# Causal mask of attention scores added in VectorE's pass for the maximum, in one core's hybrid decoder layer

## The chip, the cores and the metric

The kernel runs on one core of one Trainium2 chip, as a single program. The metric is device time in microseconds (us), the median of several runs; lower is better. A core has five engines that run at the same time and hand work to one another through semaphores: TensorE (PE in the profile, with its weight loads as PEld), VectorE (DVE), ScalarE (ACT), GpSimd (POOL) and SyncE (SP, which here only issues transfers). TensorE writes its products into PSUM, a small memory of eight banks; the other working memory is SBUF.

## What is computed

One decoder layer for a sequence of 1024 tokens of width 1024, in fp32. After a norm, one projection feeds two groups of heads side by side. Group B (gated DeltaNet, four heads) is a chunked scan along the sequence and is not touched here. Group A is differential attention: four heads, each with two softmax maps over the same causal past, and the second map subtracted with a learned weight. Both outputs go through one output projection, are added to the input, and an MLP with squared ReLU follows. The attention, cut to what matters:

```python
s = jnp.einsum('bqhcd,bkhcd->bhcqk', qb, k, preferred_element_type=jnp.float32) * scale
causal = (start + jnp.arange(Q_BLOCK))[:, None] >= k_pos[None, :]
s = jnp.where(causal, s, jnp.finfo(jnp.float32).min)
p = jax.nn.softmax(s, axis=-1)
a = p[:, :, 0] - lam * p[:, :, 1]
return jnp.einsum('bhqk,bkhe->bqhe', a.astype(v.dtype), v)
```

q and k are RMS-normed over the 64 entries of each of their parts beforehand; each head's output is RMS-normed after.

## The kernel before

The work runs in stages: the projections of the DeltaNet group with its preparation (to about 250 us), then a long stretch in which several strands are interleaved (about 250 to 625 us), then the MLP (to the end). Products in fp32 are made of three products of rounded parts (`wH`/`hH` the high part, `wL`/`hL` the rest).

The interleaved stretch is where the change lies. Its strands are generators: `scan` and `scan_out` (DeltaNet), `da_units` (projections of q, k and v of the attention, 48 units of 24 matmuls into `ps_qk`, L1063 to L1065), `da_turns` (transposes of q and k, `ps_qkt`, L1024), `scores` (the softmax maps), `values` (transposes of the maps, L1230 into `ps_at`, and their product with v, L1242 into `ps_o`), `mix_loads` and `mixed` (transposes of the mixed rows, L298), and `outproj` (L1332 to L1334). A planner, the class `Interleave`, decides at build time which strand issues next. It keeps a clock of its own for TensorE (`flow.pe`) and estimated queues of VectorE, ScalarE and GpSimd (`flow.chain` with `vec`, `act`, `powr`), and it holds a PSUM bank until the chain that reads it should be done (`flow.hold`). A strand whose bank or operand isn't due yet steps back, and another goes. TensorE's instructions then stand in exactly that order. The orders of the other engines and of the transfers are made by the framework's scheduler around it. A few transfers are tied behind another instruction by hand (`tc.issue_after`).

One unit of `scores` is one head and one block of 128 queries (`tb`), 32 units in all; it has two maps. A map has n = 128 (tb + 1) keys, from 128 to 1024, in one or two pieces of up to 512 columns, each piece in a PSUM bank of the tile `ps_sc`. There are two such tiles (`qsc`, and `rsc` once the scan is over). For each piece two matmuls run (L1189 with `qa`, L1190 with `qb`), and in the last piece a third, L1192: identity times a triangle `caus` of 0 and -1e30, both bf16, which adds the causal mask to the last 128 columns. VectorE then reduces the map to the negated maximum `mx` (L1194). ScalarE takes the exponential out of PSUM into the SBUF tile `pexp`, with `mx` as bias and the row sum as a second output (L1198). After both maps VectorE combines them (L1205 to L1208), and the unit goes on the list `ready`; a new unit starts while at most two are on it (`AHEAD = 2`).

Two places put squares aside. In `da_units`, ScalarE squares the 256 columns of a unit of q or k into an SBUF tile `qsq` (L1081) and copies the unit to `qn` (L1082); VectorE sums the squares (L1084). The bank is booked as free after the copy. In `values`, ScalarE copies the product out (L1251), squares the copy into an SBUF tile `osq2` with the sum as second output (L1252), and the bank is booked as free after the copy. GpSimd raises the sums to the power -1/2 (L291) and issues the stores of the first two heads' outputs (`mixa_d`, L1258), from a tile `om` with two buffers.

Of the kernel before, what the change touches and what calls it, by code (L numbers as in the profile page):

```python
# [9 lines left out]
F32 = mybir.dt.float32  # L10
F32R = mybir.dt.float32r
BF16 = mybir.dt.bfloat16
AF = mybir.ActivationFunctionType
ALU = mybir.AluOpType
AX = mybir.AxisListType
# [3 lines left out]
P = 128  # L19
# [88 lines left out]
def act(n, accum=False):  # L108
    return "S", 55.0 + 0.83 * n + (93.0 if accum else 0.0)


def vec(n, extra=0.0):
    return "V", 68.0 + 1.045 * n + extra


def powr(n):
    return "G", 180.0 + 285.0 * n
# [3 lines left out]
def tile_hymba_layer(  # L121
# [7 lines left out]
    V, S, G, T = nc.vector, nc.scalar, nc.gpsimd, nc.tensor  # L129
# [349 lines left out]
    with tc.manual_schedule(engines={T.engine, V.engine, S.engine, G.engine}):  # L479
# [49 lines left out]
        for tb in range(3, NT):  # L529
            for u in range(2):  # L530
                nxt, at = spread_at.get((tb, u), (None, 0))
                z[tb, u] = z_mm(tb, u, *pools[tb], nxt, at)
                if nxt is not None:
# [4 lines left out]
                    if nxt in (4, 5):  # L538
                        b = {4: 5, 5: 7}[nxt]
                        z_root(b)  # L540
                        z_diag(b)
                    last = next(parts)
# [16 lines left out]
    identb = const.tile([P, P], BF16, name="identb")  # L559
# [3 lines left out]
    caus = const.tile([P, P], BF16, name="caus")  # L563
# [8 lines left out]
    ps = ph.tile([P, 512], F32, tag="ph", name="ps_pv")  # L572
# [40 lines left out]
    u, au, e, w1, lw, d1, z1 = (n32(n) for n in ("gu", "gau", "gte", "gw1", "glw", "gd1", "gz1"))  # L613
# [21 lines left out]
    ps = ph.tile([P, 512], F32, tag="ph", name="ps_g")  # L635
# [21 lines left out]
    def ta(name, bufs, dt=F32):  # L657
        return sa.tile([P, 512], dt, tag=name, name=name, bufs=bufs)
# [100 lines left out]
    for h, hf, y, th in skew(dn_proj(1)):  # L759
# [3 lines left out]
        ps = transposed(k2)  # L763
# [65 lines left out]
    for h, hf, q2 in skew(dn_proj(0)):  # L829
# [3 lines left out]
        ps = transposed(q2)  # L833
        psm = gram(k2, q2)
        sq = ta("kn", 2)
# [15 lines left out]
    for h, hf, v2 in skew(dn_proj(2)):  # L851
        ps = transposed(v2)
# [20 lines left out]
    ap = dctx.enter_context(tc.tile_pool(name="ap", bufs=1, **right))  # L873
    sdctx = ExitStack()
    sd = sdctx.enter_context(tc.tile_pool(name="sd", bufs=1, **right))
# [2 lines left out]
    qsc = scctx.enter_context(tc.tile_pool(name="qsc", bufs=1, space=PSUM, **right))  # L878

    flow = Interleave()  # L880

    def bank_tile(pool, res, name):
        return pool.tile([P, 512], F32, tag=f"{res[0]}{res[1]}", name=name)
# [153 lines left out]
    def da_units():  # L1037
        todo = [(g, kind) for g in range(2) for kind in (1, 0, 2)]

        w = load_unit(w_units[2 * todo[0][1] + todo[0][0]]), unit_time()  # L1040
        for g, kind in todo[1:]:
            quarters.plan(w_units[2 * kind + g])
        for k0 in (4, 0):
            for n in range(2):
                quarters.plan(w_halves[n], k0, 4)
        quarters.load()
        quarters.load()
        freed = [0.0, 0.0]
        n = 0
        for i, (g, kind) in enumerate(todo):  # L1050
            (wh, wl), wt = w
            for j in range(NT):
                tb = NT - 1 - j if i == len(todo) - 1 else j
                if j == 0:
                    if i + 1 < len(todo):
                        w = quarters.unit(256, KB)
                    else:
                        pre.append(quarters.unit(512, 4))
                sl = slice(tb * P, (tb + 1) * P)
                yield max(freed[n % 2], wt[0] if j == 0 else 0.0), None  # L1060
                ps = pj.tile([P, 512], F32, tag="pj", name="ps_qk")
                for k in range(KB):
                    T.matmul(ps[:, :256], hH[:, k, sl], wh[:, k, :], start=(k == 0), stop=False)  # L1063
                    T.matmul(ps[:, :256], hH[:, k, sl], wl[:, k, :], start=False, stop=False)  # L1064
                    T.matmul(ps[:, :256], hL[:, k, sl], wh[:, k, :], start=False, stop=(k == KB - 1))  # L1065
                    if k % 2 == 1:
                        flow.pe(6 * TR)
                        if k < KB - 1:
                            yield wt[k // 2 + 1], None
                while len(late) > 2:  # L1070
                    yield flow.now + 50, None
                qn = sd.tile([P, 256], F32, tag="qn", name="qn", bufs=4)
                if kind == 2:
                    newest["ACT"] = S.copy(qn, ps[:, :256])
                    st = nc.gpsimd.dma_start(v_d[g, tb], qn.rearrange("p (h e) -> p h e", h=2))
                    if g == 1:
                        prefetch_x()
                    freed[n % 2] = flow.chain(act(256))
                else:
                    sq = sd.tile([P, 256], F32, tag="qsq", name="qsq", bufs=1)  # L1080
                    S.activation(sq, ps[:, :256], AF.Square)  # L1081
                    newest["ACT"] = S.copy(qn, ps[:, :256])  # L1082
                    sn = sd.tile([P, 4], F32, tag="sn", name="sn", bufs=2)
                    V.tensor_reduce(sn, sq.rearrange("p (a d) -> p a d", d=DQK), axis=AX.X, op=ALU.add)  # L1084
                    rn = sd.tile([P, 4], F32, tag="rn", name="rn", bufs=2)
                    rstd(rn, sn, 1.0 / DQK, EPS, sd, "rnt", 4)
                    qv = qn.rearrange("p (a d) -> p a d", d=DQK)
                    V.tensor_tensor(qv, qv, rn.unsqueeze(2).broadcast_to([P, 4, DQK]), ALU.mult)
                    t = flow.chain(act(256))
                    freed[n % 2] = flow.chain(act(256), start=t - flow.HOP)  # L1090
                    t = flow.chain(vec(256), vec(4), powr(4), vec(256), start=t - flow.HOP)
                    late.append((g, kind, tb, qn, t))
                quarters.block()
                if i == len(todo) - 1:
                    over.add(tb)
                n += 1
                state["units"] = n
            if kind == 2:
                while state["turned"] < 2 * NT * (g + 1):
                    yield flow.now + 50, None  # L1100
                state["da"] = g + 1
                state["da_t"] = flow.now + 3000
        sdctx.close()
        pctx.close()
        state["proj"] = True
# [30 lines left out]
    def scores():  # L1136
# [6 lines left out]
        for u, (h, tb) in enumerate(order):  # L1143
# [8 lines left out]
            if h == 2 and h not in heads:  # L1152
                while state["turned"] < 3 * NT:
                    yield flow.now + 300, None
                ks = load_head(2, ap), load_head(3, pools["a2"])
# [15 lines left out]
            qa, qb = q  # L1171
            n = (tb + 1) * P
            npc = 1 if n <= 512 else 2
            pl = n // npc
            pe, ssum = [], ap.tile([P, 2], F32, tag="ssum", name="ssum", bufs=4)
            mx = ap.tile([P, 2], F32, tag="mx", name="mx", bufs=4)
            for m in range(2):
                nsc += 1
                if state["scan"] and nsc % 2:
                    name, sc = "rsc", pools["rsc"]  # L1180
                else:
                    name, sc = "qsc", qsc
                yield 0, name
                sc = sc.tile([P, 1024], F32, tag="sc", name="ps_sc")
                for pc in range(npc):
                    o = sc[:, 512 * pc:512 * pc + pl]
                    ks = KS[m][:, pc * pl:(pc + 1) * pl]
                    last = pc == npc - 1
                    T.matmul(o, qa[:, m, :], ks, start=True, stop=False)  # L1189
                    T.matmul(o, qb[:, m, :], ks, start=False, stop=not last)  # L1190
                    if last:
                        T.matmul(sc[:, 512 * pc + pl - P:512 * pc + pl], identb, caus, start=False, stop=True)  # L1192
                scv = sc.rearrange("p (a b) -> p a b", b=512)[:, :npc, :pl]
                V.tensor_reduce(mx[:, m:m + 1], scv, axis=AX.XY, op=ALU.max, negate=True)  # L1194
                npe += 1
                ep = pools["be"] if state["scan"] and npe % 3 == 0 else ae
                e = ep.tile([P, SEQ], F32, tag="pexp", name="pexp")
                S.activation(e[:, :n].rearrange("p (a b) -> p a b", a=npc), scv, AF.Exp, bias=mx[:, m:m + 1],  # L1198
                             accum_out=ssum[:, m:m + 1])
                flow.pe(2 * max(n / 2.4, 110.0) + 55)  # L1200
                t = flow.chain(vec(n), act(n, True))
                flow.hold(name, t)
                pe.append(e)
            ri = ap.tile([P, 2], F32, tag="ri", name="ri", bufs=4)
            V.reciprocal(ri, ssum)  # L1205
# [3 lines left out]
            t = flow.chain(vec(10), vec(1, 60), vec(n, 100), start=t - flow.HOP)  # L1209
# [4 lines left out]
    def values():  # L1214
        for _ in order:
# [9 lines left out]
            for g in range(0, tb + 1, 4):  # L1225
# [11 lines left out]
                t = flow.chain(act(ng * P))  # L1237
                flow.hold(r, t)
            r = yield from flow.bank("px", at=t)
            po = bank_tile(px, r, "ps_o")  # L1240
            for j in range(tb + 1):
                T.matmul(po[:, :P], ats[j // 4][:, (j % 4) * P:(j % 4 + 1) * P], vt[:, j, :],  # L1242
                         start=(j == 0), stop=(j == tb))
            if h < 2:
                om = ap.tile([P, P], F32, tag="om", name="om", bufs=2)
            else:

                om = rows_of[tb][:, h * P:(h + 1) * P]
            sq = ap.tile([P, P], F32, tag="osq2", name="osq2", bufs=1)
            so = ap.tile([P, 1], F32, tag="so2", name="so2", bufs=2)  # L1250
            S.copy(om, po[:, :P])  # L1251
            S.activation(sq, om, AF.Square, scale=ri[:, 0:1], accum_out=so)  # L1252
# [7 lines left out]
            t = flow.chain(act(P))  # L1260
            flow.hold(r, t)
            t = flow.chain(act(P, True), vec(1), powr(1), vec(1), vec(P, 60), start=t)
# [568 lines left out]
    last = u_raw(4)  # L1831
# [78 lines left out]
```

## Time and profile before

| | |
|---|---|
| Median of 3 runs | 1241.6 us (1239.6 to 1242.4) |
| Profiled execution: span from first to last instruction | 1237.3 us (no time of its own is given beside it) |
| TensorE busy | 1222.9 us, 99% |
| TensorE weight loads busy | 1053.6 us, 85% |
| VectorE busy | 824.9 us, 67% |
| ScalarE busy | 618.7 us, 50% |
| GpSimd busy | 154.6 us, 12% |
| The reduction L1194, 64 times | 47.4 us, 752 ns each |
| The exponential L1198, 64 times | 47.5 us, 743 ns each |

In the profile's rows, "L1194" is a line of the kernel, an arrow points from what is read to what is written, "x64" is a count. Rows of groups give busy time, mean duration in ns, and the idle time of the engine just before, with the instruction that ended it. Rows of the timeline give start and duration in us. Rows of waits give total, count and longest. Matmul rows overlap, as matmuls are pipelined: what one costs is seen from start to start. The granted clock of TensorE is 1.000 throughout.

### The profile page before, as it was taken

What the parts mean: (1) busy time and instruction counts of PE and PEld (TensorE: products, weight loads), DVE (VectorE), ACT (ScalarE), POOL (GpSimd) and SP (SyncE); (2) the same over time, 40 slices, a digit from 0 to 9 for tenths busy, and PEclk for the clock granted to TensorE, in tenths of its full rate; (3) what the DMA queues carried; (4) which work ended last, traced back from release to release, by engine and by line L of the source; (5) the groups of instructions that cost most, each with busy time, mean ns of one, the idle gap of its engine ahead of it and who ended that gap; (6) DMA issues with size and microseconds to landing.
All of it is one profiled execution on the core that took longest, in us unless ns stands there. A gap on an engine that the chain in (4) does not pass through costs nothing.

```text
span 1237.3 us, 18898 instructions
## 1 busy us (share of the span) xinstructions
PE 1222.9 (99%) x6887; PEld 1053.6 (85%) x6887; DVE 824.9 (67%) x1458; ACT 618.7 (50%) x1249; POOL 154.6 (12%) x215
## 2 busy tenths in 40 slices
PE   9999999999999999999999999999999999999998
PEld 8978888899998998888888888888888888888886
DVE  6868796566647656777689555566569755777543
ACT  6587554244445555566667444544564333333330
POOL 2411110034335421111200000000000000000000
PEclk9999999999999999999999999999999999999999
DMA  9344653179648755223346534444469655432301
GB/s 350 104 112 119 167 158 108 56 238 270 212 141 256 219 163 151 82 72 115 125 147 223 189 122 157 180 156 153 167 234 376 237 179 186 166 102 102 137 34 68
DMA packets 143301, 202.12 MB, mean 163 GB/s; under 512 B 20920, under 2 KB 98280, under 8 KB 143208
## 3 DMA queue, kind: packets, MB, share of 16 engines
q1 hardware_dynamic: 138584, 187.28, 46.6%
q0 software_dynamic: 4480, 13.64, 2.9%
q8 instruction: 54, 0.88, 0.3%
q14 instruction: 39, 0.32, 0.1%
q10 hardware_dynamic: 144, 0.00, 0.0%
HBM read 135.86 MB, written 65.01 MB: 162 GB/s over the span
## 4 chain that ended last, share of the span: by engine, by line
PE 93%; DMA 2%; DVE 2%; ACT 1%; issue 1%; POOL 1%; DVEq 0%; SPq 0%; ACTq 0%; POOLq 0%
PE X L1509 5%; PE X L1507 5%; PE X L1508 5%; PE X L1806 4%; PE X L1805 4%; PE X L1807 4%; PE ps_dn L265 3%; PE ps_dn L267 3%; PE ps_dn L266 3%; PE ps_qk L1063 3%; PE ps_qk L1064 3%; PE ps_qk L1065 3%; PE Y L1507 3%; PE Y L1509 2%; PE Y L1508 2%; PE ps_op L1332 2%
## 5 line engine op out<-in xcount | busy, mean ns | idle before, releaser
L1425 ACT CAST hH<-ur 128x1024 fp32r<-128x1024 f32 x56 | 58.9, 1051 | 173.2 <-PE Y L1806 89.4
L1426 DVE TENSOR_TENSOR hL<-ur,hH 128x1024 fp32r<-128x1024 f32 x56 | 68.4, 1223 | 79.8 <-ACT hH L1425 79.7
L1063 PE MATMUL ps_qk<-wH,hH 128*128 128x256 f32 x384 | 114.6, 299 | 0.1
L1065 PE MATMUL ps_qk<-wH,hL 128*128 128x256 f32 x384 | 108.6, 283 | 0.0
L1064 PE MATMUL ps_qk<-wL,hH 128*128 128x256 f32 x384 | 108.4, 282 | 0.0
L1426 DVE TENSOR_TENSOR op<-raw,op 128x1024 fp32r<-128x1024 f32 x48 | 58.7, 1223 | 74.2 <-PE X L1508 41.2
L1805 PE MATMUL X<-hH 128*128 128x512 f32 x224 | 87.1, 389 | 0.0
L1806 PE MATMUL X<-hL,hH 128*128 128x512 f32 x224 | 87.1, 389 | 0.0
L1807 PE MATMUL X<-hH,hL 128*128 128x512 f32 x224 | 87.1, 389 | 0.0
L265 PE MATMUL ps_dn<-hH,wH 128*128 128x512 f32 x192 | 76.3, 397 | 0.2 <-ACT cp L678 0.2
L267 PE MATMUL ps_dn<-hH,wL 128*128 128x512 f32 x192 | 75.8, 396 | 0.0
L266 PE MATMUL ps_dn<-hL,wH 128*128 128x512 f32 x192 | 75.8, 395 | 0.0
L1063 PEld LDWEIGHTS ps_qk<-wH,hH 128*128 128x128 f32 x384 | 73.4, 191 | 0.3 <-ACT qn L1082 0.2
L1064 PEld LDWEIGHTS ps_qk<-wL,hH 128*128 128x128 f32 x384 | 73.4, 191 | 0.0
L1065 PEld LDWEIGHTS ps_qk<-wH,hL 128*128 128x128 f32 x384 | 73.1, 190 | 0.0
L1426 DVE TENSOR_TENSOR hL<-dw,hH 128x1024 fp32r<-128x1024 f32 x56 | 68.2, 1218 | 0.9 <-ACT hH L1425 0.9
L1425 ACT CAST op<-raw 128x1024 fp32r<-128x1024 f32 x48 | 50.4, 1052 | 35.7 <-PE Y L1509 19.9
L1425 ACT CAST hH<-dw 128x1024 fp32r<-128x1024 f32 x56 | 58.7, 1048 | 10.8 <-DMA dw<-in_w_down_dram 5.1
L1198 ACT ACTIVATE pexp<-ps_sc,mx 128x128 f32<-128x128 f32 (+7 forms) x64 | 47.5, 743 | 30.4 <-DVE mx L1194 30.0
L682 DVE SCALAR_TENSOR_TENSOR cy<-cp,pv,cy 128x512 f32<-128x512 f32 x72 | 53.7, 746 | 8.3 <-ACT cy L680 7.5
L1332 PE MATMUL ps_op<-wH,hH 128*128 128x512 f32 x128 | 54.7, 427 | 0.0
L1194 DVE TENSOR_REDUCE mx<-ps_sc 128x1 f32<-128x128 f32 (+7 forms) x64 | 47.4, 752 | 10.6 <-PE ps_sc L1192 10.0
(368 smaller groups left out, 3452.8 us busy)
## 6 DMA issues: line engine op xcount, KB each, us to landing
ur<-ud SPq DMA_DIRECT2D x28, 1024.0 KB, 4.9
raw<-in_w_up_dram SPq DMA_DIRECT2D x32, 512.0 KB, 3.9
dw<-in_w_down_dram SPq DMA_DIRECT2D x32, 512.0 KB, 7.2
wraw<-in_w_units_dram SPq DMA_DIRECT2D x48, 256.0 KB, 3.8
qk_d<-qa POOLq DMA_DIRECT2D x32, 256.0 KB, 3.9
ud<-ua SPq DMA_DIRECT2D x16, 512.0 KB, 4.5
ud<-s SPq DMA_DIRECT2D x16, 512.0 KB, 2.7
pka<-park_d SPq DMA_DIRECT2D x32, 192.0 KB, 4.2
```

The costliest lines, as they stand in the source:

```text
L265: T.matmul(ps, lh(k), rh(k), start=(k == 0), stop=False)
L266: T.matmul(ps, lh(k), rl(k), start=False, stop=False)
L267: T.matmul(ps, ll(k), rh(k), start=False, stop=(k == n - 1))
L1063: T.matmul(ps[:, :256], hH[:, k, sl], wh[:, k, :], start=(k == 0), stop=False)
L1064: T.matmul(ps[:, :256], hH[:, k, sl], wl[:, k, :], start=False, stop=False)
L1065: T.matmul(ps[:, :256], hL[:, k, sl], wh[:, k, :], start=False, stop=(k == KB - 1))
L1425: S.copy(dst[0], src)
L1426: V.tensor_tensor(dst[1], src, dst[0].bitcast(F32), ALU.subtract)
L1507: T.matmul(ps, op[0][:, k, cs], h[0][:, k, :], start=start and k == 0, stop=False, skip_group_check=True)
L1805: T.matmul(bank[t], v[0][:, j, sl], v[2][:, j], start=s0, stop=False, skip_group_check=True)
L1806: T.matmul(bank[t], v[0][:, j, sl], v[3][:, j], start=False, stop=False, skip_group_check=True)
L1807: T.matmul(bank[t], v[1][:, j, sl], v[2][:, j], start=False, stop=s1, skip_group_check=True)
```

## The change

The mask matmul L1192 goes. A tile `mk` of 640 bf16 columns is made once: 512 zeros and then the triangle. Its last n columns (or, for a map in two pieces, a piece of zeros and the last columns) are the second operand of one fused VectorE instruction, which computes -(scores + mask) into the SBUF tile `pexp` and at the same time its minimum over the row into `mx`. The exponential then runs in place in SBUF, with a scale of -1 and that minimum as bias. The planner's estimates follow: TensorE's time for a map loses 55 ns, VectorE's gains 60, and the score bank is held until VectorE's pass and not until the exponential.

The squares of both places move from SBUF tiles into free columns of the PSUM bank that they are taken from (`ps[:, 256:512]` and `po[:, P:2 * P]`). In `da_units` the planner now books the bank until VectorE has summed the squares; in `values` its booking stays.

```diff
     flow = Interleave()
+    MK = 512 + P
+    mk = ap.tile([P, MK], BF16, name="mk")
+    V.memset(mk[:, 0:512], 0.0)
+    V.tensor_copy(mk[:, 512:MK], caus)
...
-                    sq = sd.tile([P, 256], F32, tag="qsq", name="qsq", bufs=1)
+                    sq = ps[:, 256:512]
                     S.activation(sq, ps[:, :256], AF.Square)
                     newest["ACT"] = S.copy(qn, ps[:, :256])
...
                     t = flow.chain(act(256))
-                    freed[n % 2] = flow.chain(act(256), start=t - flow.HOP)
-                    t = flow.chain(vec(256), vec(4), powr(4), vec(256), start=t - flow.HOP)
+                    flow.chain(act(256), start=t - flow.HOP)
+                    freed[n % 2] = t = flow.chain(vec(256), start=t - flow.HOP)
+                    t = flow.chain(vec(4), powr(4), vec(256), start=t - flow.HOP)
...
-                    last = pc == npc - 1
                     T.matmul(o, qa[:, m, :], ks, start=True, stop=False)
-                    T.matmul(o, qb[:, m, :], ks, start=False, stop=not last)
-                    if last:
-                        T.matmul(sc[:, 512 * pc + pl - P:512 * pc + pl], identb, caus, start=False, stop=True)
-                scv = sc.rearrange("p (a b) -> p a b", b=512)[:, :npc, :pl]
-                V.tensor_reduce(mx[:, m:m + 1], scv, axis=AX.XY, op=ALU.max, negate=True)
+                    T.matmul(o, qb[:, m, :], ks, start=False, stop=True)
                 npe += 1
                 ep = pools["be"] if state["scan"] and npe % 3 == 0 else ae
                 e = ep.tile([P, SEQ], F32, tag="pexp", name="pexp")
-                S.activation(e[:, :n].rearrange("p (a b) -> p a b", a=npc), scv, AF.Exp, bias=mx[:, m:m + 1],
+                scv, ev, mv = sc[:, :n], e[:, :n], mk[:, MK - n:]
+                if npc == 2:
+                    scv = sc.rearrange("p (a b) -> p a b", b=512)[:, :, :pl]
+                    ev = ev.rearrange("p (a b) -> p a b", a=2)
+                    mv = bass.AP(mk.tensor, mk.offset, [[MK, P], [MK - pl, 2], [1, pl]])
+                V.tensor_tensor_reduce(ev, scv, mv, -1.0, 3.0e38, ALU.add, ALU.min, mx[:, m:m + 1])
+                S.activation(e[:, :n], e[:, :n], AF.Exp, scale=-1.0, bias=mx[:, m:m + 1],
                              accum_out=ssum[:, m:m + 1])
-                flow.pe(2 * max(n / 2.4, 110.0) + 55)
-                t = flow.chain(vec(n), act(n, True))
+                flow.pe(2 * max(n / 2.4, 110.0))
+                t = flow.chain(vec(n, 60))
                 flow.hold(name, t)
+                t = flow.chain(act(n, True), start=t - flow.HOP)
                 pe.append(e)
...
-            sq = ap.tile([P, P], F32, tag="osq2", name="osq2", bufs=1)
+            sq = po[:, P:2 * P]
             so = ap.tile([P, 1], F32, tag="so2", name="so2", bufs=2)
             S.copy(om, po[:, :P])
             S.activation(sq, om, AF.Square, scale=ri[:, 0:1], accum_out=so)
```

## The prediction

> **What bounds the kernel now.** I read the page first: the busy times and the chain that ended last.
>
> ```profile
> span 1237.3 us, 18898 instructions
> ...
> PE 1222.9 (99%) x6887; PEld 1053.6 (85%) x6887; DVE 824.9 (67%) x1458; ACT 618.7 (50%) x1249; POOL 154.6 (12%) x215
> ...
> PE 93%; DMA 2%; DVE 2%; ACT 1%; issue 1%; POOL 1%; DVEq 0%; SPq 0%; ACTq 0%; POOLq 0%
> ```
>
> TensorE is busy for all but 1% of the span and makes 93% of the chain. So an edit counts by what it takes from or adds to TensorE's stream of instructions, and by the waits it makes there. The edit lives in the middle of the kernel, so next come the stages from the first block of projection (250) to the last output projection (625); columns are stage, its length, then the busy time of PE, PEld, DVE, ACT and POOL.
>
> ```profile
> 250.00:355.00 105.00, 103.59 (x896) 102.44 (x895) 62.95 (x190) 46.12 (x141) 41.74 (x54) 1.00 0.73 231
> 355.00:460.00 105.00, 101.81 (x830) 97.08 (x830) 65.11 (x174) 60.17 (x169) 43.63 (x61) 1.00 0.70 206
> 460.00:580.00 120.00, 119.86 (x742) 101.17 (x741) 88.01 (x197) 72.38 (x197) 16.26 (x26) 1.00 0.38 102
> 580.00:625.00 45.00, 44.32 (x225) 36.91 (x224) 31.10 (x64) 28.50 (x68) 11.01 (x14) 1.00 0.46 159
> ```
>
> TensorE idles 1.41 + 3.19 + 0.14 + 0.68 = 5.4 us in these 375 us, at the full granted clock (the 1.00). VectorE and ScalarE have a third and more of their time free. What little TensorE waits for, in all of 200 to 700:
>
> ```profile
> PE ps_o L966 <- DMA pkb<-park_d: 1.3, 1, 1.3
> PE ps_at L1230 <- DVE qa L1029: 0.9, 1, 0.9
> PE ps_at L1230 <- ACT om L1251: 0.8, 1, 0.8
> PE ps_tr L1438 <- ACT hn L1439: 0.7, 1, 0.7
> PE ps_qkt L1024 <- DVE ri L1205: 0.6, 1, 0.6
> PE ps_sc L1189 <- ACT pexp L1198: 0.6, 1, 0.6
> ```
>
> Single waits of about a microsecond, none of them systematic. After 625 TensorE has no gap up to the last microseconds, so what is saved before arrives at the end whole.
>
> **The mask matmuls go: 64 matmuls and 64 weight loads off TensorE.** The cost of one is not its duration (its rows overlap the neighbours') but how far it pushes the next starts apart. Two score maps back to back, where the upper pair of rows has no mask between and the lower has one:
>
> ```profile
> 474.52 0.37 PE L1190 MATMUL ps_sc<-KS,qb 128*128 128x448 f32 x1
> 474.73 0.37 PE L1189 MATMUL ps_sc<-KS,qa 128*128 128x448 f32 x1
> 474.94 0.37 PE L1190 MATMUL ps_sc<-KS,qb 128*128 128x448 f32 x1
> 475.15 0.23 PE L1192 MATMUL ps_sc<-caus,identb 128*128 128x128 bf16 x1
> 475.19 0.45 PE L1189 MATMUL ps_sc<-KS,qa 128*128 128x448 f32 x1
> 475.48 0.37 PE L1190 MATMUL ps_sc<-KS,qb 128*128 128x448 f32 x1
> ```
>
> From a qb to the next qb: 474.94 - 474.52 = 0.42 us without, 475.48 - 474.94 = 0.54 us with the mask. One mask costs 0.12 us: 0.04 its own slot (475.15 to 475.19), 0.08 because the matmul after it is held longer (0.29 to the next start against 0.21), two weight loads now having to fit in front of it. Where plain transposes follow, only a wider slot of 0.07 is left, as at the first mask; the last is of the dear kind:
>
> ```profile
> 359.80 0.23 PE L1192 MATMUL ps_sc<-caus,identb 128*128 128x128 bf16 x1
> 359.87 0.28 PE L1024 MATMUL ps_qkt<-ident,qn 128*128 128x128 f32 x1
> 359.98 0.27 PE L1025 MATMUL ps_qkt<-ident,qn 128*128 128x128 f32 x1
> ```
> ```profile
> 575.22 0.23 PE L1192 MATMUL ps_sc<-caus,identb 128*128 128x128 bf16 x1
> ```
>
> Counting what follows each of the 64 along the timeline, 53 stand before a large matmul (L1189, L1332, L1063, L1242) and 11 before a transpose: 53 x 0.12 + 11 x 0.07 = 7.1 us. Bounds: 64 x 0.04 = 2.6 (only the slot comes back) and 64 x 0.12 = 7.7. I take 7.1, the rows' own count. The Trainium skill (TensorE: Matmul & The Clock Gate, section Back-to-back issue gap) gives N / 2.4 + 2.5 ns for an isolated matmul; as an estimate by that page one mask is 56 ns and all of them 3.6 us, and the sum below would be a gain of 3.0 us.
>
> **The fused pass on VectorE.** The order of the changed program has two instructions for each map in place of the reduction: the pass itself, and one that fetches the minimum. Nothing of that form runs in the kernel before, so its nearest rows: the old reduction, an addition of one PSUM and one SBUF operand, and an operation on two SBUF operands.
>
> ```profile
> L1339 DVE TENSOR_TENSOR acc<-acc,ps_op 128x512 f32<-128x512 f32 x31 | 21.2, 683 | 9.5 <-PE ps_op L1334 8.7 <-DMA qa<-qk_d 0.6
> ...
> L1194 DVE TENSOR_REDUCE mx<-ps_sc 128x1 f32<-128x1024 f32 x8 | 9.6, 1215 | 0.2 <-PE ps_sc L1192 0.2
> ...
> L1208 DVE SCALAR_TENSOR_TENSOR pexp<-pexp,cf 128x1024 f32<-128x1024 f32 x4 | 5.1, 1284 | 0.0
> ...
> L1194 DVE TENSOR_REDUCE mx<-ps_sc 128x1 f32<-128x128 f32 x8 | 2.3, 290 | 2.4 <-PE ps_sc L1192 2.3
> ```
>
> The reduction grows by (1215 - 290) / 896 = 1.03 ns per element, so at 512 it stands at 686 ns; the addition takes 683. A second operand and an output stream thus cost nothing extra in the nearest row, and I take the pass at the reduction's time. The fetch I bound by zero and by ScalarE's own fetch of a sum:
>
> ```profile
> L1251 ACT COPY om<-ps_o 128x128 f32<-128x128 f32 x16 | 4.2, 266 | 12.5 <-PE ps_o L1242 7.7 <-DMA mixa_d<-om 4.7
> ...
> L1252 ACT ACTIVATION_READ_ACCUMULATOR osq<-om,ri 128x1 f32 x16 | 3.1, 193 | 0.0
> ```
>
> At 0.19 us it is 64 x 0.19 = 12 us of VectorE. From 355 to 580 VectorE is busy 65.1 + 88.0 = 153 of 225 us, which becomes 165: beside TensorE's work, and the planner lets scores run two finished units ahead of their transposes, so 0.4 us per unit is covered. Without that cover it would be 32 units x 0.4 = 12 us. Price taken: nothing. The exponential now reads SBUF and not PSUM; it sits behind the same VectorE pass on an engine with more room still, also nothing.
>
> **The score bank is free after VectorE's pass, not after the exponential.** That ends the wait of L1189 for pexp: 0.6 us gained. The next thing late there is the pass itself, far shorter than the two engines in a row.
>
> **Squares go to PSUM banks.** In the attention output the square now writes into the bank of the product, so the bank comes free not after the copy (0.27) but after the square and its fetch, 0.40 + 0.19 = 0.59 us later:
>
> ```profile
> L1252 ACT ACTIVATE osq<-om,ri 128x128 f32<-128x128 f32 x16 | 6.4, 403 | 0.3
> ```
>
> The planner still books the bank as free after the copy. By the changed program's order and PSUM addresses, 5 of the 32 outputs have only 5 to 8 small matmuls before TensorE writes that bank again (0.11 us each by the rows at 359.87 and 359.98, so 0.6 to 0.9 us); the rest have more. Between 0 and 5 x 0.59 = 3.0 us; I take 1.0, since the copy begins at once in most places. In the projections of q and k the bank is now held until VectorE's reduction of the squares. The shortest cover I find after the first unit:
>
> ```profile
> 421.04 0.41 DVE L1084 TENSOR_REDUCE sn<-qsq 128x4 f32<-128x256 f32 x1
> ```
> ```profile
> 422.91 0.36 PE L1063 MATMUL ps_qk<-wH,hH 128*128 128x256 f32 x1
> ```
>
> The reduction ends 1.46 us before TensorE takes the bank again, so this costs nothing, but for the first unit, whose bank is retaken as soon as it is free: between 0 and the 0.41 of the reduction, 0.2 taken. The mask tile's fill and copy are two VectorE instructions in front of a stage with a third of it idle: nothing.
>
> **The sum.** -7.1 - 0.6 + 1.0 + 0.2 = -6.5 us. The profiled execution gives a span of 1237.3 and no time of its own; the runs (1239.6 to 1242.4) lie 2.3 to 5.1 above it, the median 4.3. A span of 1230.8 puts the median at 1241.6 - 6.5 = 1235.1 us.
>
> **Rivals.** The planner writes TensorE's order from estimated times, and with other estimates the order differs from the first projection block on, as do the orders of VectorE, ScalarE, POOL and SP's loads.
> *The new order waits more.* If TensorE's idle time of 5.4 us doubles, the gain shrinks to 1.1 us: 1240.5. For it: the largest waits hang on chance meetings. Against: they have no common cause that the edit feeds. Chance 0.12.
> *The new order misses an old stall.* One wait stands behind three rows of the list above: a copy on ScalarE stood for 4.68 us until a store issued seven microseconds earlier had landed and its buffer came free.
>
> ```profile
> 379.53 0.54 POOL L1258 DMA_DIRECT2D mixa_d<-om  x1 [1.53 <-DVE rnt L290]
> ```
> ```profile
> 386.47 0.27 ACT L1251 COPY om<-ps_o 128x128 f32<-128x128 f32 x1 [4.68 <-DMA mixa_d<-om]
> ```
>
> Everything behind it on ScalarE's queue was late, and TensorE waited for om and qa (0.8 + 0.9) and, as I read it, for the backlog at ri (0.6): 2.3 us. If outputs stand further apart this goes: 1235.1 - 2.3 = 1232.8. The edit doesn't address it. Chance 0.10.
> *Only the slot comes back.* If the matmul behind a mask is late for another reason than the two loads, the masks give 2.6 us: -2.6 - 0.6 + 1.2 = -2.0, that is 1239.6. The pair 0.21 and 0.29 speaks against it. Chance 0.06; by the TensorE page's isolated gap, 1238.6.
> *The fused pass runs at half rate: slower.* Each map then costs VectorE another 1.03 ns per element; the maps hold 8 x (128 + 256 + ... + 1024) = 36,864 elements per partition, 38 us. VectorE would stand at 153 + 12 + 38 = 203 of 225 us from 355 to 580, and scores, the additions of the output projection and the norms queue behind it. Between none and all of it lands on TensorE; with a third, 12.7 us, the time is 1235.1 + 12.7 = 1247.8. It decides from 9.0 us on TensorE (the gain and 2.5 more), 27 us on VectorE, which is a pass of 1024 elements at 1.215 + 0.75 = 1.97 us or more. For it: the operation is a new one with an accumulator. Against: L1339, and L1208 with two SBUF operands at 1284 ns, show no halving. The Trainium skill (Vector Engine (DVE) Microarchitecture Reference, section Points that are easy to get wrong) warns that scalar-tensor-tensor forms with two SBUF sources that are not bf16 run at half throughput, as no port is left for the accumulator; here one source is PSUM and the mask is bf16, and L1208, which has two such sources but no accumulator, does not show it. Chance 0.12.
> That the edit does not take effect is excluded: the changed program holds no mask matmul.
>
> **How the numbers follow.** My forecast has 0.60. Its ends: all masks at 0.12, no bank waits and the old stall gone give 1235.1 - 0.6 - 1.2 - 2.3 = 1231.0; doubled waits with 1.5 us more for the banks give 1242.0. I leave out the half-rate case and little else: 1231.0 to 1242.0. A measurement of this kernel can tell about 0.2%, 2.5 us, from no change: faster, below 1239.1, takes the forecast, the missed stall and 0.03 of the two small-gain cases, 0.73; the rest of those is same, 0.14; slower has the half-rate case and the far end of the waits, 0.13.
>
> **What would show it.** Right: TensorE's starts around two score maps 0.42 us apart everywhere; the fused pass near 1.2 us at 1024 elements with a fetch under 0.2; TensorE's idle time between 250 and 625 at 4 to 7 us; the stages after 625 unchanged in length. Wrong: a pass near 2 us; waits of ps_at or ps_qkt for om or for the squares adding up to more than 3 us; a long wait for a store or a load that the new order has placed badly.

## The result

The changed kernel takes 1235.41 us (median of 6 runs, 1234.16 to 1236.54) against 1240.97 us for the kernel before on the same chip (6 runs, 1239.6 to 1244.93): ratio 0.9955, 95% interval 0.9941 to 0.9969. That is 5.6 us less (3.8 to 7.3). The forecast was 6.5 us less.

The page of the changed kernel: the span, the busy times, and the chain that ended last. New lines shift the line numbers: L1193 and L1194 are now the two score matmuls, L1204 the fused pass, L1205 the exponential, L1259 and L1260 the copy and the square of the attention output.

```profile
span 1233.0 us, 18819 instructions
...
PE 1217.3 (99%) x6823; PEld 1054.3 (86%) x6823; DVE 824.7 (67%) x1524; ACT 624.2 (51%) x1249; POOL 151.3 (12%) x215
...
PE 88%; DVE 4%; DMA 3%; ACT 2%; issue 2%; POOL 1%; SPq 1%; POOLq 0%; DVEq 0%; ACTq 0%
```

TensorE has 64 matmuls less (6823 for 6887) and stays the bound. The same four stages of the interleaved stretch:

```profile
250.00:355.00 105.00, 101.56 (x881) 100.22 (x880) 62.11 (x190) 45.67 (x138) 41.05 (x53) 1.00 0.73 227
355.00:460.00 105.00, 103.35 (x840) 100.97 (x839) 66.59 (x201) 64.27 (x175) 43.43 (x63) 1.00 0.71 211
460.00:580.00 120.00, 118.89 (x713) 104.15 (x712) 89.65 (x242) 75.58 (x199) 14.52 (x27) 1.00 0.38 103
580.00:625.00 45.00, 44.26 (x230) 36.98 (x229) 33.11 (x64) 29.85 (x67) 10.44 (x13) 1.00 0.51 177
```

TensorE idles 3.44 + 1.65 + 1.11 + 0.74 = 6.9 us, 1.5 more than before (5.4), inside the 4 to 7 that the prediction named. The largest waits of TensorE from 200 to 700 are other ones than before:

```profile
PE ps_qkt L1028 <- DVE qn L1092: 1.3, 2, 1.0
PE ps_o L970 <- DMA pkb<-park_d: 1.2, 1, 1.2
PE ps_qkt L1028 <- ACT ps_o L1260: 1.1, 2, 0.8
PE ps_at L1238 <- ACT ps_o L1260: 0.8, 2, 0.7
PE ps_qkt L1028 <- ACT qn L1086: 0.8, 1, 0.8
PE ps_tr L298 <- POOL hn L1370: 0.7, 1, 0.7
PE ps_sc L1194 <- DMA qb<-qk_d: 0.5, 1, 0.5
```

The wait for om is gone, and that of the score matmul for the exponential. Two new rows, 1.1 and 0.8 us, are waits for a PSUM bank until the output's square (ACT ps_o L1260) has been written into it. Where the masks stood, the score matmuls follow one another evenly:

```profile
471.23 0.36 PE L1194 MATMUL ps_sc<-KS,qb 128*128 128x448 f32 x1
471.43 0.36 PE L1193 MATMUL ps_sc<-KS,qa 128*128 128x448 f32 x1
471.63 0.37 PE L1194 MATMUL ps_sc<-KS,qb 128*128 128x448 f32 x1
471.84 0.37 PE L1193 MATMUL ps_sc<-KS,qa 128*128 128x448 f32 x1
472.05 0.37 PE L1194 MATMUL ps_sc<-KS,qb 128*128 128x448 f32 x1
```

From qb to qb it is 0.40 and 0.42 us in these rows, where the place with a mask took 0.54. The fused pass, its fetch of the minimum, and the exponential from SBUF, by groups of one shape:

```profile
L1204 DVE CUSTOM_DVE_ANT_1 pexp<-ps_sc,mk 128x1024 f32<-128x1024 f32 x8 | 9.8, 1222 | 0.2 <-PE ps_sc L1194 0.2
L1205 ACT ACTIVATE pexp<-pexp,mx 128x1024 f32<-128x1024 f32 x8 | 9.2, 1153 | 5.9 <-DVE mx L1204 5.9
...
L1204 DVE DVE_READ_ACCUMULATOR2_ANT mx<- 128x1 f32 x64 | 5.3, 83 | 0.0
```

The pass takes 1222 ns at 1024 elements, the reduction's 1215 within 1%, and the fetch 83 ns.

### The profile page after: what moved, and what is told of

Its sections match the earlier page's. It is cut to its first block, busy times and chain, and to the rows that moved or that the text cites. A ratio compares the mean times of both kernels' runs of the same rounds, so it can differ in the third digit from the quotient of the medians.

```text
span 1233.0 us, 18819 instructions
## 1 busy us (share of the span) xinstructions
PE 1217.3 (99%) x6823; PEld 1054.3 (86%) x6823; DVE 824.7 (67%) x1524; ACT 624.2 (51%) x1249; POOL 151.3 (12%) x215
## 3 DMA queue, kind: packets, MB, share of 16 engines
q1 hardware_dynamic: 138584, 187.28, 46.9%
## 4 chain that ended last, share of the span: by engine, by line
PE 88%; DVE 4%; DMA 3%; ACT 2%; issue 2%; POOL 1%; SPq 1%; POOLq 0%; DVEq 0%; ACTq 0%
PE X L1517 4%; PE X L1515 4%; PE X L1516 4%; PE X L1814 4%; PE X L1815 4%; PE X L1813 4%; PE ps_dn L265 3%; PE ps_dn L267 3%; PE ps_dn L266 3%; PE ps_qk L1067 3%; PE ps_qk L1068 3%; PE ps_qk L1069 3%; PE ps_o L1250 2%; PE Y L1515 2%; PE Y L1517 2%; PE Y L1516 2%
## 5 line engine op out<-in xcount | busy, mean ns | idle before, releaser
L1205 ACT ACTIVATE pexp<-pexp,mx 128x128 f32<-128x128 f32 (+7 forms) x64 | 49.7, 777 | 25.1 <-DVE mx L1204 24.5
L1515 PE MATMUL Y<-hH,op 128*128 128x512 f32 x128 | 49.9, 390 | 0.4 <-DVE ua L1555 0.4
```

What stands on the lines that cost most here:

```text
L1515: T.matmul(ps, op[0][:, k, cs], h[0][:, k, :], start=start and k == 0, stop=False, skip_group_check=True)
```

## The experiments

Every run was timed beside the kernel before on the same chip. All ratios are to that kernel; in us they are multiplied by 1240. "Old" estimates are the planner's of the kernel before. The squares of the projections are in SBUF in e1, e2 and e14, and in PSUM in all other rows.

| Run | Masks | Output's square | Planner: projections, scores | Ratio (95% interval) | us against before |
|---|---|---|---|---|---|
| changed kernel | fused pass | PSUM | new, new | 0.9955 (0.9941 to 0.9969) | -5.6 |
| e1_no_mask | none | SBUF | old, old | 0.9951 (0.9938 to 0.9963) | -6.1 |
| e2_two_masks | two matmuls | SBUF | old, old | 1.0021 (1.0012 to 1.0030) | +2.6 |
| e14_out_squares_alone | matmul | PSUM | old, old | 1.0049 (1.0036 to 1.0062) | +6.1 |
| e4_squares_only | matmul | PSUM | new, old | 1.0070 (1.0058 to 1.0082) | +8.7 |
| e3_old_estimates | fused pass | PSUM | old, old | 1.0029 (1.0019 to 1.0040) | +3.6 |
| e12_score_estimates | fused pass | PSUM | old, new | 1.0000 (0.9991 to 1.0010) | 0.0 |
| e6_bank_booked | fused pass | PSUM, booked | new, new | 0.9973 (0.9961 to 0.9984) | -3.3 |
| e9_old_estimates_sbuf | fused pass | SBUF | old, old | 0.9957 (0.9945 to 0.9970) | -5.3 |
| e10_score_estimates_sbuf | fused pass | SBUF | old, new | 0.9992 (0.9983 to 1.0002) | -1.0 |
| e11_proj_estimates_sbuf | fused pass | SBUF | new, old | 0.9997 (0.9987 to 1.0006) | -0.4 |
| e5_out_squares_sbuf | fused pass | SBUF | new, new | 0.9969 (0.9957 to 0.9980) | -3.8 |
| e7_extra_pass | fused pass, one more pass | PSUM | new, new | 1.0146 (1.0132 to 1.0160) | +18.1 |

**The masks alone, taken away (e1) and doubled (e2).** TensorE's order of all other matmuls is that of before in both.

```diff
 e1:
-                    T.matmul(o, qb[:, m, :], ks, start=False, stop=not last)
-                    if last:
-                        T.matmul(sc[:, 512 * pc + pl - P:512 * pc + pl], identb, caus, start=False, stop=True)
+                    T.matmul(o, qb[:, m, :], ks, start=False, stop=True)
 e2:
-                        T.matmul(sc[:, 512 * pc + pl - P:512 * pc + pl], identb, caus, start=False, stop=True)
+                        for i in range(2):
+                            T.matmul(sc[:, 512 * pc + pl - P:512 * pc + pl], identb, caus, start=False, stop=i == 1)
```

> The kernel before without its 64 mask matmuls, nothing put in their place, so the attention is not causal; planner's estimates and TensorE's order of all other matmuls are as before. Theory (a mask costs the starts it pushes apart, 0.12 or 0.07 us): 7.1 us less than before, ratio 0.994, starts in a run of score matmuls 0.42 us apart per pair. Rival (only the slot of 0.04 us comes back): 2.6 us less, ratio 0.998.

> The kernel before with each mask matmul issued twice (masked scores reach -2e30, the softmax is the same); planner and order as before. Theory (the weight loads in front of the next matmul set the price): 6 to 8 us more than before, ratio 1.005 to 1.0065. Rival (only the slot): 2.6 to 3.5 us more, ratio 1.002 to 1.003.

Measured: without masks 6.1 us less (4.6 to 7.7), which holds the 7.1 of the theory and not the 2.6 of the slot alone. By the two pages it is TensorE's stream that got shorter: its busy time is 1217.2 us against 1222.9, and its idle time in the span is the same to about 0.1. Doubled, only 2.6 us more (1.5 to 3.7): the theory of e2 missed, and the number of its rival came out. The timeline of e2, the counterpart of the place that the prediction read:

```profile
475.62 0.36 PE L1190 MATMUL ps_sc<-KS,qb 128*128 128x448 f32 x1
475.83 0.28 PE L1193 MATMUL ps_sc<-caus,identb 128*128 128x128 bf16 x2
475.92 0.45 PE L1189 MATMUL ps_sc<-KS,qa 128*128 128x448 f32 x1
476.21 0.37 PE L1190 MATMUL ps_sc<-KS,qb 128*128 128x448 f32 x1
```

From qb to qb it is now 0.59 us: 0.42 without a mask, 0.54 with one, 0.59 with two. The matmul behind the masks is held 0.29 us to the next start, exactly as behind one. So the 0.08 us is paid once behind the masks, and not for each weight load; a second small matmul adds 0.05 us. 64 x 0.05 is 3.2, inside the interval. That it is the change from a small matmul to a large one, and nothing peculiar to the mask or to bf16, is shown by the kernel before at a place without a mask, where a projection follows a transpose of 128 columns in fp32:

```profile
367.89 0.27 PE L1025 MATMUL ps_qkt<-ident,qn 128*128 128x128 f32 x1
367.92 0.36 PE L1063 MATMUL ps_qk<-wH,hH 128*128 128x256 f32 x1
368.12 0.28 PE L1064 MATMUL ps_qk<-wL,hH 128*128 128x256 f32 x1
368.24 0.28 PE L1065 MATMUL ps_qk<-wH,hL 128*128 128x256 f32 x1
```

The first large matmul is held 0.20 us to the next start, the second 0.12: the same 0.08. The Trainium skill (TensorE: Matmul & The Clock Gate, section Back-to-back issue gap) has N / 2.4 + 2.5 ns for a matmul by itself, as an estimate 56 ns for 128 columns, and says that this counts too little in a stream, where it states 81 ns measured. The second mask's price here, 0.05 us, is near the first of the two figures; the first mask's, 0.12, is above both.

**The squares in PSUM, alone (e14) and with the projections' new booking (e4).** e14 keeps the order of before and has a single edit; e4 has all edits on squares.

```diff
 e14, and in e4 beside the qsq edit and its booking:
-            sq = ap.tile([P, P], F32, tag="osq2", name="osq2", bufs=1)
+            sq = po[:, P:2 * P]
```

> The kernel before with one edit: the square of the attention output goes into the product's PSUM bank. TensorE's order is exactly that of before, in which 10 of the 32 outputs have at most 8 small matmuls before TensorE writes the bank again (5 in the changed kernel's order). Theory (this edit was the loss on the old order): 4 to 8 us more than before, waits of ps_at for the square of 4 us or more. Rival (it hurt only together with the fused pass): within 2 us of before.

> The kernel before with only the squares moved into PSUM, and the planner's booking of the projection bank as in the changed kernel; masks stay as matmuls. Theory (the bank that is free 0.56 us later costs a few single waits): 1 to 3 us more than before. Rival (covered everywhere): no change.

e14 is 6.1 us slower (4.5 to 7.7), as its theory had it. Its list of TensorE's waits from 200 to 700:

```profile
PE ps_at L1230 <- ACT ps_o L1252: 5.8, 6, 1.5
PE ps_o L966 <- DMA pkb<-park_d: 2.2, 3, 1.5
PE ps_qkt L1024 <- ACT ps_o L1252: 1.2, 3, 0.6
...
PE ps_tr L298 <- ACT ps_o L1252: 0.4, 1, 0.4
```

Waits for the square, 5.8 + 1.2 + 0.4 = 7.4 us, that the list of before has not. e4 was expected at 1 to 3 us and is 8.7 slower (7.2 to 10.2), so its theory and its rival missed; its own list has 4.2 + 1.1 + 0.2 = 5.5 us of these waits and more for pkb. In its profiled execution the granted clock was 0.98 from 250 to 355 us, as an estimate 2 us (0.02 x 105); the rest of its loss is not accounted for.

**The fused pass on the old order (e3, e9).** Both have the planner's old estimates, so the order of before without masks, but for a few places among small matmuls.

```diff
 e3:
-                    flow.chain(act(256), start=t - flow.HOP)
-                    freed[n % 2] = t = flow.chain(vec(256), start=t - flow.HOP)
-                    t = flow.chain(vec(4), powr(4), vec(256), start=t - flow.HOP)
+                    freed[n % 2] = flow.chain(act(256), start=t - flow.HOP)
+                    t = flow.chain(vec(256), vec(4), powr(4), vec(256), start=t - flow.HOP)
...
-                flow.pe(2 * max(n / 2.4, 110.0))
-                t = flow.chain(vec(n, 60))
+                flow.pe(2 * max(n / 2.4, 110.0) + 55)
+                t = flow.chain(vec(n), act(n, True))
                 flow.hold(name, t)
-                t = flow.chain(act(n, True), start=t - flow.HOP)
 e9, the same and:
-            sq = po[:, P:2 * P]
+            sq = ap.tile([P, P], F32, tag="osq2", name="osq2", bufs=1)
```

> The changed kernel with the planner's estimates of before, so TensorE's order is that of before without the masks, but for 26 places among small matmuls at the start of the interleaved stretch. Theory (the gain is the masks; the re-estimated order only shuffles single waits): within 2 us of the changed kernel, 1234 to 1237. Rival (the new estimates carry a part of the gain): 2 to 4 us above the changed kernel. Rival on the other side (the new order has added waits): 1 to 3 us below it.

> The run with the old estimates, with the square of the attention output back in its SBUF tile; same TensorE order as that run, nearly the order of before. Theory (its loss was the bank held through the square, 6.1 us of waits in its list): 5 to 6 us less than that run, so 3 us below before and 2 us above the changed kernel. Rival (the fused pass with its two instructions on VectorE costs on the old order): at most 2 us less than that run.

e3 was the surprise: 3.6 us slower than before, so 9.2 us slower than the changed kernel (0.0074 x 1240). Its theory and both rivals missed it; that the new estimates carry a part of the gain was the nearest. Its first row of waits:

```profile
PE ps_at L1236 <- ACT ps_o L1258: 5.3, 6, 1.8
```

With the rows of ps_tr and ps_qkt (0.4 each) these are 6.1 us. e9, in the same order with the square back in SBUF, is at -5.3 us: 8.9 less than e3, where 5 to 6 were expected, and level with the changed kernel. (In the two profiled executions the difference is smaller, spans of 1239.5 and 1234.5 us.) So on the old order the square's place costs 6 to 9 us, and everything else of the change (fused pass, projections' squares in PSUM, exponential from SBUF) takes away little of the masks' gain: -5.3 against -6.1 for e1, intervals overlapping.

**The square back in SBUF on the new order (e5), and booked (e6).**

```diff
 e5: the second edit of e9 alone, on the changed kernel
 e6:
-            t = flow.chain(act(P))
+            t = flow.chain(act(P), act(P, True))
             flow.hold(r, t)
-            t = flow.chain(act(P, True), vec(1), powr(1), vec(1), vec(P, 60), start=t)
+            t = flow.chain(vec(1), powr(1), vec(1), vec(P, 60), start=t)
```

> The changed kernel with the square of the attention output back in its SBUF tile (the projections' squares stay in PSUM); TensorE's order is exactly that of the changed kernel. Theory (the bank held through the square makes the waits of ps_qkt and ps_at for that square, 1.1 and 0.8 us): 1.5 to 2 us less than the changed kernel, and those two rows gone. Rival (something else is late right behind): no change.

> The changed kernel with the planner told that the bank of an attention output is held through the square and its sum. TensorE's order differs from the changed kernel's from the first output on. Theory (the planner steers around a wait that it knows of): waits for the square under 0.5 us, time 1 to 2 us less than the changed kernel. Rival (any new order moves single waits about): between 2 us less and 5 us more, with other waits in the list.

Neither is better than the changed kernel: -3.8 and -3.3 against -5.6 us, intervals overlapping. Both theories missed and both rivals came out. In e5, whose order is the changed kernel's, both rows for the square are gone, but 0.7 of the 1.9 us comes back as the first row below, a wait of the same transposes for the copy, with small ones elsewhere. e6's list keeps one wait for the square, the second row below, and has new ones for at, hL and of. Its order was a new draw, as its rival said.

```profile
PE ps_qkt L1028 <- ACT om L1259: 0.7, 1, 0.7
```
```profile
PE ps_qkt L1028 <- ACT ps_o L1260: 1.0, 1, 1.0
```

**Which estimates made the order (e12, e10, e11).** e12 has the old projections' lines of e3 and the new scores' lines, e10 the same with the square in SBUF, e11 the new projections' and the old scores' lines with the square in SBUF.

> The changed kernel with the planner's estimates of before in the projections and the new ones in the scores; squares in PSUM. Theory (the new order's gain comes from the scores' estimates, by which the score bank is free earlier and both maps of a unit go out together): within 2 us of the changed kernel. Rival (it comes from the projections' booking): 5 to 8 us above it, as with all estimates old.

> The same with the square of the attention output in SBUF, as a candidate for a better version. Theory (the changed kernel's waits of ps_qkt for qn at 283 and 302 us, 1.3 and 0.8 us, come from the projections' new estimates; the masks are gone, and no bank is held through a square): 1 to 3 us less than the changed kernel. Rival (single waits only move): within 1.5 us of it.

> The last of four combinations with the output's square in SBUF: the planner's new booking in the projections and its old estimates in the scores; no mask matmuls, fused pass. Theory (the projections' booking takes away TensorE's idle time in 355 to 460 us, 5.5 to 5.8 with the old and 1.7 with the new, and gives back 2 in 250 to 355): idle 3 to 4 us in 250 to 355 and under 3 in 355 to 460; 2 to 4 us less than before's time minus nothing for the scores, that is 1234 to 1237, as with all estimates new. Rival (each new order is a new draw of single waits): anywhere from 1232 to 1241, with idle in 355 to 460 not tied to the booking.

All three theories missed in time. e12 lies 5.6 us above the changed kernel, a number that its rival had. Its waits for the square are down to 0.9 + 0.7 + 0.2 = 1.8 us from e3's 6.1, and it is 3.6 faster than e3: the new order removes most of those waits, but TensorE still idles 5.6 us from 355 to 460, where the changed kernel idles 1.7. e10 and e11 lose 4.6 and 5.2 us to the changed kernel though no bank waits for a square in them. TensorE's rows for 355 to 460, in order e9, e10, e11, e5:

```profile
355.00:460.00 105.00, 99.19 (x802) 96.44 (x802) 64.69 (x196) 61.62 (x168) 42.49 (x60) 1.00 0.70 206
```
```profile
355.00:460.00 105.00, 99.46 (x793) 96.83 (x792) 62.99 (x189) 60.36 (x163) 41.17 (x59) 0.98 0.67 204
```
```profile
355.00:460.00 105.00, 101.47 (x826) 99.30 (x825) 65.18 (x197) 63.21 (x171) 43.60 (x62) 1.00 0.70 209
```
```profile
355.00:460.00 105.00, 103.27 (x839) 100.89 (x838) 65.09 (x200) 63.16 (x173) 43.80 (x63) 1.00 0.71 211
```

Idle there: 5.8, 5.5, 3.5 and 1.7 us; the projections' new booking takes away 2.3 of it with the scores' old estimates and 3.8 with the new. But e9, with the most, is the fastest of the four in time, and e10 and e11 are the slowest: the idle time of this one stage does not rank them. With the square in SBUF, the four combinations span 5 us, -5.3 to -0.4, and the two re-estimates don't add up. Each order is a draw of single waits.

A single wait can also cost more than its length. In the second row above, e10's, the granted clock is 0.98 and not 1.00. Cut finer, that is one wait of 2.3 us (ps_qkt for qn) and then 3.4 us at half the clock:

```profile
393.00:396.20 3.20, 0.86 (x8) 0.69 (x7) 2.11 (x7) 1.88 (x4) 2.41 (x4) 1.00 0.93 253
396.20:399.60 3.40, 3.40 (x18) 3.40 (x17) 1.52 (x4) 1.30 (x4) 0.95 (x2) 0.50 0.96 352
399.60:403.00 3.40, 3.40 (x29) 3.37 (x28) 0.58 (x2) 1.05 (x4) 0.64 (x2) 1.00 1.01 389
```

A second such stretch lies at 311 us, behind two waits for pkb (1.6 us together). By the pages, e10's span is 6.2 us longer than the changed kernel's; 4.1 of that are the same 6823 matmuls taking longer (busy 1221.4 against 1217.3), and only 2.1 idle time. Not every long wait is followed by this: e3 has one of 1.8 us, and e7 one of 3.3 us at 469 us, with the full clock behind it. What decides is not shown, but it adds to the draw.

**How much VectorE can take (e7).**

```diff
                 V.tensor_tensor_reduce(ev, scv, mv, -1.0, 3.0e38, ALU.add, ALU.min, mx[:, m:m + 1])
-                S.activation(e[:, :n], e[:, :n], AF.Exp, scale=-1.0, bias=mx[:, m:m + 1],
+                V.tensor_reduce(mx2[:, m:m + 1], ev, axis=AX.XY if npc == 2 else AX.X, op=ALU.min)
+                S.activation(e[:, :n], e[:, :n], AF.Exp, scale=-1.0, bias=mx2[:, m:m + 1],
```

> The changed kernel with one more VectorE reduction over each map between the fused pass and the exponential, some 47 us of VectorE in all, which is what the fused pass at half rate and a little more would have cost; TensorE's order is unchanged. The prediction's price (a third of it reaches TensorE): 15 us more than the changed kernel. Rival (covered by the two units ahead): under 4 us more. Rival (all of it): 40 us or more.

The eight shapes of the added reduction take 46.9 us in all, and the kernel is 23.7 us slower than the changed one (0.0191 x 1240): half of it shows in the time, not a third, and the rivals (under 4, 40 or more) are out. By the pages, 17.6 us of that are idle time of TensorE (33.3 against 15.7 of the span), which is a little over a third of the pass. Another 5.7 are the same 6823 matmuls taking longer (busy 1223.0 against 1217.3): the granted clock fell to half in two stretches behind long waits, and all five executions have a mean of 0.993 to 0.997. The stage that suffers most is the one where VectorE has the least room; TensorE idles 13.0 us in it, 1.1 in the changed kernel:

```profile
460.00:580.00 120.00, 107.04 (x636) 94.18 (x635) 100.04 (x223) 62.60 (x155) 13.84 (x23) 0.97 0.32 90
```

Its longest waits are all for VectorE:

```profile
PE ps_at L1240 <- DVE pexp L1218: 6.8, 3, 3.3
PE ps_at L1240 <- DVE ri L1215: 5.4, 2, 4.7
PE ps_qkt L1028 <- DVE rnt L290: 2.7, 1, 2.7
```

## Why the prediction was right

**The masks.** 7.1 us was the rows' count; e1 gives 6.1 (4.6 to 7.7). Reading start to start in one place with and one without a mask was enough, and the rival of the slot alone (2.6) is out. The cause that the prediction gave, two weight loads in front of the next matmul, does not hold as it stands: two masks put three loads there, and the next matmul waits no longer. What is paid for is the change from a small matmul to a large one, whatever the small one is; why that takes 0.08 us is open.

**The fused pass.** Sized at the reduction's time; it is that, to 7 ns at 1024 elements. The fetch was bounded by 0.19 us and is 0.083. The rival of the half rate is out. The warning of the Trainium skill (Vector Engine (DVE) Microarchitecture Reference, section Points that are easy to get wrong) is for two SBUF sources that are not bf16; with one PSUM and one bf16 source this trace shows no halving, and nothing here tried two such sources with an accumulator. The price in that rival was too low: by e7, as an estimate, half of 38 us, 19, would have landed. One reading behind it was wrong: the prediction gave VectorE a third and more of its time free, but from 460 to 580 its own row leaves 32 of 120 us, 27%, and that is where e7 lost most.

**The score bank.** The wait for the exponential is gone, 0.6 us, as forecast.

**The squares' bank.** 1.0 us taken of 0 to 3.0; the changed kernel's rows have 1.9, and taking the cause away (e5) gains nothing that can be measured. The size holds for this order alone: I had counted 5 close places in it. In the old order there are 10 of them, and the same edit costs 6.1 us (e14), or 8.9 beside the fused pass (e9 to e3).

**The projections' bank.** Sized at 0.2 for real waits of the bank. No wait of a projection for VectorE's sum is in the changed kernel's list (e10 and e12, whose planner does not know of the longer hold, have one of 0.7 us); what came there are 1.3 + 0.8 us of the transposes L1028 for qn, which are placed earlier than qn is ready.

**The order.** Here the prediction was lucky. It took the new order as neutral and gave 0.12 to its waiting more. Measured, new estimates were worth -9.2 us where the square is in PSUM (e3 to the changed kernel) and about +1.5 where it is in SBUF (e9 to e5, intervals overlapping), where one of the two new estimates alone cost 4.3 and 5.0 (e9 to e10 and to e11). Of the eight versions with the fused pass in the table that differ only in estimates, booking and the square's place, four gain more than 0.2%, three lie within 0.2% and one is slower. By that count the prediction should have given faster about 0.5 rather than 0.73. The planner did not do it knowingly: told of the bank (e6), it does no better. Why the order of the changed kernel is among the best of these stays open.

In sum, step by step: masks -6.1 (e1), the rest of the change on the old order 0.8 (e1 to e9), square's place 8.9 (e9 to e3), new order -9.2 (e3 to the changed kernel). That is -5.6 by construction, as each step starts where the one before ends. Taken the other way round, the new order is 1.5 (e9 to e5) and the square's place -1.8 (e5 to the changed kernel), neither clear of noise. So the two have no price of their own, only together. The forecast's -6.5 has the same first term, and its small bank term fits the order that happened to come out. That the forecast time, 1235.1 us, lies so near the measured 1235.4 is luck in part: it starts from 1241.6, the median of three runs, and six have 1240.97.

## What to carry to other kernels

Price a small matmul among large ones from start to start and not by its row or its columns: here 0.12 us for one of 128 columns, and 0.05 for a second one in the same place. Scratch output in the accumulator's bank saves SBUF but makes the bank's release wait for one more engine operation; whether that costs nothing or 9 us depends on how soon TensorE comes back to the bank, so count the close returns in the order that will run. Where a planner makes the order from estimates, time an edit on the old order and on the new one apart, as the order alone moved this kernel by several us either way. And read the granted clock of each stage beside TensorE's idle time: a long wait can leave a stretch at half the clock behind it.

## What the runs showed of the hardware

The fetch of a reduction's result on VectorE takes 83 ns, less than half of ScalarE's fetch of its sum (187 to 211 ns here). The exponential takes 1153 ns from SBUF against 1118 from PSUM at 1024 elements, and 398 against 366 at 128: some 35 ns for each instruction. The square of 128 elements takes 373 ns into PSUM against 403 into SBUF; the Trainium skill (ScalarE: Activation LUTs, section Step-by-step: what each stage is for) says that ScalarE writes faster to PSUM, and the 30 ns agree, though the longer hold of the bank cost far more in e14 (6.1 us). The first large matmul behind a small one is held 0.08 us longer than the next, behind a bf16 mask as behind an fp32 transpose. Behind a wait of TensorE of 2.3 us the granted clock was 0.50 for 3.4 us in e10; the projections' matmuls of 256 columns, else 0.12 us apart, start 0.21 us apart in such a stretch (e10 at 312 us).
